# The last step of a masked-autoencoder loss: 32 sums as a row on one partition instead of a column on 32

## The chip, the cores and the metric

The kernel runs on one core of a Trainium2 chip. A core has five engines that work at the same time, each with its own queue of instructions: TensorE (PE in the profile; its weight loads are PEld), VectorE (DVE), ScalarE (ACT), GpSimd (POOL) and SyncE (SP). DMA transfers between the chip's main memory (DRAM) and the on-chip memory SBUF run on sixteen DMA engines; an instruction on SyncE or GpSimd starts them. SBUF, and PSUM, into which TensorE writes, have 128 partitions (rows). The metric is the device time of one execution in microseconds (us).

## The reference

`pred` and `target` are float32 of shape (32, 147, 768): 32 batches of 147 masked patches.

```python
mean = target.mean(axis=-1, keepdims=True)
var = target.var(axis=-1, keepdims=True)
target = (target - mean) / np.sqrt(var + 1e-6)
loss = np.mean((pred - target) ** 2, axis=-1)
return loss.mean(axis=-1).astype(np.float32)
```

The output is 32 float32 numbers, one mean for each batch, 128 bytes in all. The inputs are 28.9 MB.

## The kernel before, in words

The 147 patches of a batch are spread over four partitions, so that 32 batches fill 128 partitions. Each partition takes 37 consecutive patches, except that a batch's fourth partition takes 36. So there are 36 chunks in which all 128 partitions hold a patch (chunk c is the c-th patch of every partition), and one more, the rest, in which 96 partitions do.

Loads (line 89) bring one, two or four chunks at a time. The first two of `target` go through SyncE's queue in float32, all others through GpSimd's, which turns them into bfloat16 on the way. Then, for each chunk:

- `stats` on VectorE gives mean and variance of each patch (lines 140 and 141); ScalarE takes a square root (142), and VectorE makes the factor `r` and the offset `nmr` of it (143, 144);
- `normalise` on GpSimd writes the normalised target `s` (158);
- `subtract` on TensorE forms `p - s` in PSUM as two products with the identity and the negated identity (178). It works on units: the rest, then 17 pairs of chunks, then the last two chunks one by one. PSUM has two buffers `z` for this;
- `square` on ScalarE squares a unit in place and adds up each partition's row (184). The sum goes into one column of `rl` (128 partitions x 19 units), or into `rl_rest` for the rest.

What is left is to add, for each batch, its four partitions and its 19 columns. `mask` is 128 x 32: it holds 1/(147*768) where partition and batch belong together, and 0 elsewhere; `mask_rest` is the same for the 96 partitions of the rest. `sums` (188, 190) multiplies them on TensorE into one PSUM tile `acc`. The first fifteen columns go in one product, as soon as they are there (the early sums), then the rest, then the four last columns one by one, added to column 0 of `acc`:

```python
pin(nc.tensor.matmul(acc[:, 0:b - a], mask, rl[:, a:b], start=a == 0, stop=b == len(main_units)))
```

In `matmul(out, w, x)` the operand `w` is loaded into the array and `x` is streamed through it; the result has a partition for each column of `w` and a column for each column of `x`. So `acc` has 32 partitions and 15 columns. VectorE adds up its columns into `ob` (line 224), 32 partitions of one number, and SyncE stores them (line 225). The lines at the end of the program (256) are closing waits that the framework adds: every engine waits until all DMAs have landed.

The order in which an engine gets its instructions is set by a plan in the code: a small model of landing times and engine speeds gives each step a due time, and the steps are written out in that order and kept in it (`pin`). The plan puts the early sums and the rest's at 71.78 (three units after the square of the last of those columns), between the square of the pair (32, 33) at 70.78 and that of chunk 34 at 72.43; the last statistics stand at 63.60.

Of the kernel before, what the change touches and what calls it, by code (L numbers as in the profile page):

```python
# [7 lines left out]
F32 = mybir.dt.float32  # L8
BF16 = mybir.dt.bfloat16
ALU = mybir.AluOpType  # L10
# [4 lines left out]
def kernel(  # L15
# [7 lines left out]
    nc = tc.nc  # L23
    pin = tc.keep_in_program_order
    B, N, D = pred.shape
    eps = 1e-6
    P = 128
# [4 lines left out]
    RP = B * (J - 1)  # L32
# [17 lines left out]
    singles = ctx.enter_context(tc.tile_pool(name="singles", bufs=1))  # L50
    psum = ctx.enter_context(tc.tile_pool(name="psum", bufs=2, space=bass.MemoryType.PSUM))
    psum1 = ctx.enter_context(tc.tile_pool(name="psum1", bufs=1, space=bass.MemoryType.PSUM))
# [52 lines left out]
    mask = singles.tile([P, B], F32)  # L105
    mask_rest = singles.tile([P, B], F32)
# [55 lines left out]
    main_units = [u for u in units if u[0] != REST]  # L162
    early = len(main_units) - 4
    rl = singles.tile([P, len(main_units)], F32)
    rl_rest = singles.tile([P, 1], F32)
    acc = psum1.tile([B, early], F32)
    zs = {}

    def subtract(u):
# [14 lines left out]
        pin(nc.scalar.activation(out=z[:n, :W], in_=z[:n, :W], func=ACTF.Square, accum_out=to))  # L184

    def sums(a, b):
        if a == "rest":
            pin(nc.tensor.matmul(acc[:, 0:1], mask_rest[:RP], rl_rest[:RP], start=False, stop=False))
        else:
            pin(nc.tensor.matmul(acc[:, 0:b - a], mask, rl[:, a:b], start=a == 0, stop=b == len(main_units)))  # L190

    dve = pool = pe = act = 0.0
    ready = {}
# [11 lines left out]
    for u in units:  # L205
        pe = max([pe, free[0]] + [ready[c] for c in u] + [land["p", c] for c in u])
        at(pe, lambda u=u: subtract(u))
        pe += 0.7 * len(u)
        act = max(act, pe + 0.3)
        at(act, lambda u=u: square(u))  # L210
        act += 0.65 * len(u) + 0.35
        free = [free[1], act]
        i = main_units.index(u) if u in main_units else -1
        if i == early - 1:
            at(act + 3.0, lambda: sums(0, early))
            at(act + 3.0, lambda: sums("rest", None))
        elif i >= early:
            at(act + (3.1 if i < len(main_units) - 1 else 5.0), lambda i=i: sums(i, i + 1))
# [1 line left out]
    for when, order, fn in sorted(todo, key=lambda e: e[:2]):  # L220
        fn()

    ob = singles.tile([B, 1], F32)
    nc.vector.tensor_reduce(out=ob, in_=acc, axis=mybir.AxisListType.X, op=ALU.add)  # L224
    nc.sync.dma_start(out=out, in_=ob[:, 0])


# [33 lines left out]
```

## Time and profile before

| what | us |
|---|---|
| median of three runs (lowest to highest) | 81.42 (81.22 to 82.11) |
| profiled execution: its own time | 80.73 |
| profiled execution: span, first to last instruction | 79.0 |
| VectorE busy | 45.7 |
| ScalarE busy | 32.5 |
| GpSimd busy | 50.1 |
| TensorE busy, matmul | 38.7 |
| HBM read | 28.90 MB, 366 GB/s over the span |

The span is counted from the profiled execution's first instruction. A row of a timeline gives the start in us, the duration, the engine, the line of the code, the operation, what it writes and reads and how many instructions are merged, and in brackets how long the engine had been idle and what ended that. A row of the chain of waits gives start, duration and what the chain went through. `SPq` stands for SyncE's own instruction queue. In a row of groups stand, behind a bar, busy time, mean duration in ns, and the idle time before with what ended it. The granted clock of TensorE is 1.00 in the last stretch up to 76 us.

### The profile page before, as it was taken

To read this page: it belongs to the slowest core of one execution; us is meant where nothing else is said; L and a number is where in the kernel's file an instruction comes from. 1 tells how busy PE (TensorE), PEld (TensorE's weight loads), DVE (VectorE), ACT (ScalarE), POOL (GpSimd) and SP (SyncE) were. 2 spreads that over 40 slices of the span, in tenths; PEclk is the share of its full clock that TensorE was granted. 3 is DMA by queue.
4 is the path that set the end of the run, shared out by engine and by line. 5 is a ranking of instruction groups with operands and counts; after the bars stand their busy time and mean duration, and the time that the engine had idled before them with its cause. 6 is when DMAs were issued, how large, how long until landed. Compare 5 with 4: busy or idle time off the path is not lost.

```text
span 79.0 us, 602 instructions
## 1 busy us (share of the span) xinstructions
PE 38.7 (49%) x126; PEld 13.4 (17%) x126; DVE 45.7 (58%) x137; ACT 32.5 (41%) x53; POOL 50.1 (63%) x73
## 2 busy tenths in 40 slices
PE   0000330008990069985317980991399496496500
PEld 0000210001320023231102320320131031223300
DVE  0061039979799799797797089529779267000000
ACT  5000000050100590872931760583134873999700
POOL 4998802059789899897797795399779360800000
PEclk9999999999999655599965569759956999999996
DMA  0799999999999999999999999999999999990000
GB/s 0 182 412 317 311 218 218 211 218 218 211 215 218 211 216 218 211 211 218 218 211 215 218 215 209 221 215 211 205 227 202 210 210 220 199 165 4 0 0 0
DMA packets 3444, 15.43 MB, mean 195 GB/s; under 512 B 432, under 2 KB 784, under 8 KB 3312
## 3 DMA queue, kind: packets, MB, share of 16 engines
q0 software_dynamic: 3136, 13.52, 84.2%
q1 hardware_dynamic: 304, 1.87, 6.2%
q14 instruction: 3, 0.02, 0.1%
q8 instruction: 1, 0.02, 0.1%
HBM read 28.90 MB, written 0.00 MB: 366 GB/s over the span
## 4 chain that ended last, share of the span: by engine, by line
DMA 42%; DVE 31%; ACT 7%; POOL 5%; PE 4%; issue 4%; SPq 1%; ACTq 0%
DMA p<-in_pred_dram 30%; DVE st L140 23%; DMA t<-in_target_dram 12%; DVE mv L141 5%; ACT z L184 5%; POOL s L158 5%; PE z L178 4%; ACT r L142 2%; DVE r L143 1%; DVE nmr L144 1%; SPq L89 1%; POOL t L89 1%; PE acc L190 0%; DVE ob L224 0%; ACTq L256 0%
## 5 line engine op out<-in xcount | busy, mean ns | idle before, releaser
L140 DVE BATCH_NORM_STATS2 st<-t 128x6 f32<-128x384 bf16 (+2 forms) x74 | 36.3, 533 | 14.4 <-DMA t<-in_target_dram 14.4
L158 POOL TENSOR_SCALAR s<-t,r,nmr 128x768 bf16<-128x768 bf16 (+2 forms) x37 | 35.9, 976 | 13.3 <-DVE nmr L144 13.0
L178 PE MATMUL z<-s,nident 128*128 128x512 bf16 (+3 forms) x57 | 21.4, 492 | 26.6 <-POOL s L158 23.7
L184 ACT ACTIVATE z<-z 128x1536 f32<-128x1536 f32 (+2 forms) x20 | 26.7, 1336 | 2.0 <-PE z L178 2.0
L178 PE MATMUL z<-p,ident 128*128 128x512 bf16 (+3 forms) x57 | 20.6, 478 | 8.9 <-DMA p<-in_pred_dram 8.9
L142 ACT ACTIVATE r<-mv,eps_t 128x4 f32<-128x4 f32 (+2 forms) x12 | 3.6, 296 | 39.4 <-DVE mv L141 39.4
L178 PEld LDWEIGHTS <-nident 128*128 128x128 bf16 (+1 forms) x57 | 5.8, 117 | 39.5 <-ACT z L184 16.3
L89 POOL DMA_DIRECT2D p<-in_pred_dram x13 | 7.7, 594 | 5.2 <-DMA t<-in_target_dram 3.2
L178 PEld LDWEIGHTS <-ident 128*128 128x128 bf16 (+1 forms) x57 | 7.0, 123 | 20.5 <-issue 17.8
L141 DVE BATCH_NORM_AGGREGATE mv<-st 128x2 f32<-128x12 f32 (+1 forms) x37 | 7.7, 208 | 1.3
L89 POOL DMA_DIRECT2D t<-in_target_dram x9 | 5.3, 589 | 0.0
L143 DVE RECIPROCAL r<-r 128x4 f32<-128x4 f32 (+2 forms) x12 | 2.1, 172 | 4.6 <-ACT r L142 4.6
L224 DVE TENSOR_REDUCE ob<-acc 32x1 f32<-32x15 f32 x1 | 0.2, 161 | 7.9 <-PE acc L190 7.9
L184 ACT ACTIVATION_READ_ACCUMULATOR z<-z 128x1 f32 (+1 forms) x20 | 3.7, 186 | 0.0
L144 DVE SCALAR_TENSOR_TENSOR nmr<-mv,r 128x4 f32<-128x4 f32 (+2 forms) x12 | 1.9, 161 | 0.4
L142 ACT ACT_TABLE_LOAD x1 | 1.3, 1283 | 0.8 <-PEq L242 0.8
L190 PE MATMUL acc<-rl,mask 128*32 128x1 f32 (+1 forms) x10 | 0.8, 179 | 0.8 <-ACT z L184 0.8
L190 PEld LDWEIGHTS acc<-rl,mask 128*32 128x32 f32 x10 | 0.5, 110 | 1.5 <-ACT z L184 0.9
L110 DVE MEMSET eps_t<- 128x1 f32 x1 | 0.1, 59 | 0.9 <-PEq L242 0.9
L112 POOL MEMSET ident<- 128x128 bf16 x1 | 0.4, 362 | 0.0
L113 POOL TENSOR_SCALAR_AFFINE_SELECT ident<-ident 128x128 bf16<-128x128 bf16 x1 | 0.3, 292 | 0.1
L113 POOL TENSOR_SCALAR_AFFINE_SELECT nident<-nident 128x128 bf16<-128x128 bf16 x1 | 0.3, 292 | 0.1
(13 smaller groups left out, 2.0 us busy)
## 6 DMA issues: line engine op xcount, KB each, us to landing
t<-in_target_dram POOLq DMA_DIRECT2D x7, 768.0 KB, 26.0
p<-in_pred_dram POOLq DMA_DIRECT2D x7, 768.0 KB, 26.6
t<-in_target_dram SPq DMA_DIRECT2D x1, 1536.0 KB, 9.7
p<-in_pred_dram POOLq DMA_DIRECT2D x3, 384.0 KB, 21.8
t<-in_target_dram POOLq DMA_DIRECT2D x2, 384.0 KB, 25.9
p<-in_pred_dram POOLq DMA_DIRECT2D x2, 192.0 KB, 16.4
t<-in_target_dram SPq DMA_DIRECT2D x1, 288.0 KB, 3.7
p<-in_pred_dram POOLq DMA_DIRECT2D x1, 144.0 KB, 3.7
```

The source lines that it names most:

```text
L89: pin(eng.dma_start(out=til[:n], in_=dram(x, c0, c1)))
L112: pin(nc.gpsimd.memset(til, 0.0))
L113: pin(nc.gpsimd.affine_select(out=til, in_=til, compare_op=ALU.not_equal, fill=v, base=0, pattern=[[-1, P]], channel_multiplier=1))
L140: pin(nc.vector.bn_stats(out=st[:n, j, :], in_=til[:n, o + j * half:o + (j + 1) * half]))
L141: pin(nc.vector.bn_aggr(out=mv[:n, i], in_=st[:n]))
L142: pin(nc.scalar.activation(out=r[:n], in_=mv[:n, :, 1], func=ACTF.Sqrt, bias=eps_t[:n], scale=1.0))
L143: pin(nc.vector.reciprocal(out=r[:n], in_=r[:n]))
L144: pin(nc.vector.scalar_tensor_tensor(out=nmr[:n], in0=mv[:n, :, 0], scalar=-1.0, in1=r[:n], op0=ALU.mult, op1=ALU.mult))
L158: pin(nc.gpsimd.tensor_scalar(out=s[:n, so:so + D], in0=til[:n, o:o + D], scalar1=r, scalar2=nmr, op0=ALU.mult, op1=ALU.add))
L178: pin(nc.tensor.matmul(z[:n, a:b], w[:n, :n], src[:n, so + a:so + b], start=first, stop=not first))
L184: pin(nc.scalar.activation(out=z[:n, :W], in_=z[:n, :W], func=ACTF.Square, accum_out=to))
L190: pin(nc.tensor.matmul(acc[:, 0:b - a], mask, rl[:, a:b], start=a == 0, stop=b == len(main_units)))
```

## The change

The product with the mask is turned around: the column of sums is loaded as the weight and the mask is streamed. The result then has one partition and 32 columns. Since a weight with fifteen columns would give fifteen partitions, the fifteen early columns are first added up on VectorE into one column `rl_sum`, and the first product waits for that. The last step on VectorE becomes a plain copy of one row from PSUM to SBUF, and the store reads one partition.

```diff
-    acc = psum1.tile([B, early], F32)
+    rl_sum = singles.tile([P, 1], F32)
+    acc = psum1.tile([1, B], F32)
...
         if a == "rest":
-            pin(nc.tensor.matmul(acc[:, 0:1], mask_rest[:RP], rl_rest[:RP], start=False, stop=False))
+            pin(nc.tensor.matmul(acc, rl_rest[:RP], mask_rest[:RP], start=False, stop=False))
+        elif a == 0:
+            pin(nc.vector.tensor_reduce(out=rl_sum, in_=rl[:, 0:b], axis=mybir.AxisListType.X, op=ALU.add))
+            pin(nc.tensor.matmul(acc, rl_sum, mask, start=True, stop=False))
         else:
-            pin(nc.tensor.matmul(acc[:, 0:b - a], mask, rl[:, a:b], start=a == 0, stop=b == len(main_units)))
+            pin(nc.tensor.matmul(acc, rl[:, a:b], mask, start=False, stop=b == len(main_units)))
...
-    ob = singles.tile([B, 1], F32)
-    nc.vector.tensor_reduce(out=ob, in_=acc, axis=mybir.AxisListType.X, op=ALU.add)
-    nc.sync.dma_start(out=out, in_=ob[:, 0])
+    ob = singles.tile([1, B], F32)
+    nc.vector.tensor_copy(out=ob, in_=acc)
+    nc.sync.dma_start(out=out, in_=ob[0, :])
```

## The prediction

> **What bounds the kernel now.** I read the page's totals first, then the end of the chain of waits, then everything that touches the output.
>
> ```profile
> span 79.0 us, 602 instructions
> DMA 42%; DVE 31%; ACT 7%; POOL 5%; PE 4%; issue 4%; SPq 1%; ACTq 0%
> ```
>
> The profiled execution took 80.73 us: its span of 79.0 and 1.73 around it. It lies 0.69 below the median of 81.42, so I work out a difference on this execution and apply it to the median. The first 72 us of the chain are loads and the engines that follow them, and no edit touches them. What the change can move is the end, from the last square on:
>
> ```profile
> 73.80 0.80 ACT z L184
> 74.59 0.12 ACTq L256
> 74.71 0.04 issue
> 74.75 0.24 PE acc L190 x2
> 74.99 0.02 issue
> 75.02 0.16 DVE ob L224
> ```
>
> Nothing runs in parallel here: square, product, reduction, each waiting for the one before. The reduction ends at 75.18, and the span at 79.0, so 3.82 us (4.8% of the span) belong to storing 128 bytes and closing down. The instruction queue of SyncE, its waits and the landing of the store say how they divide, and a table by stretches shows that no engine works meanwhile (columns: stretch, its length, busy time of PE, PEld, DVE, ACT and POOL, granted clock, DMA share, GB/s):
>
> ```profile
> 75.20 0.37 SPq L225 DMA_DIRECT2D out_dram<-ob  x1
> SPq L256 <- DMA out_dram<-ob: 2.2, 1, 2.2
> DMA to landing us min/median/max: 2.9/2.9/2.9
> ...
> 75.18:76.06 0.88, 0.00 (x0) 0.00 (x0) 0.00 (x0) 0.00 (x0) 0.00 (x0) 1.00 0.00 0
> 76.06:76.24 0.18, 0.00 (x0) 0.00 (x0) 0.00 (x0) 0.00 (x0) 0.00 (x0) 1.00 0.13 1
> 76.24:78.10 1.86, 0.00 (x0) 0.00 (x0) 0.00 (x0) 0.00 (x0) 0.00 (x0) 0.87 0.00 0
> 78.10:79.00 0.90, 0.00 (x0) 0.00 (x0) 0.00 (x0) 0.00 (x0) 0.00 (x0) 0.50 0.00 0
> ```
>
> Landing is at 75.20 + 2.9 = 78.10. So 0.88 us pass from the reduction's end to the first packet (0.37 of them the issue), 0.18 with packets moving, 1.86 with no packet moving and SyncE waiting, and 0.90 of closing down. The 1.86 us is the largest piece. The DMA queues between 76.0 and 76.4 (each digit is 0.01 us) show what was sent:
>
> ```profile
> DMA  0000000232100121211011000000000000000000
> DMA packets 48, 0.00 MB, mean 0 GB/s; under 512 B 48, under 2 KB 48, under 8 KB 48
> q1 hardware_dynamic: 48, 0.00, 5.8%
> ```
>
> Forty-eight packets: 32 words and 16 more, one completion for each of 16 DMA engines. Is 1.86 us what any DMA needs from its last packet to its landing? The last load answers: its issue, its size and time to landing, and the packet counts of 71.7 to 71.8 and of 71.8 to 72.4:
>
> ```profile
> 57.23 0.58 POOL L89 DMA_DIRECT2D p<-in_pred_dram  x1
> p<-in_pred_dram POOLq DMA_DIRECT2D x1, 192.0 KB, 14.9
> DMA packets 1, 0.00 MB, mean 0 GB/s; under 512 B 1, under 2 KB 1, under 8 KB 1
> DMA packets 0, 0.00 MB, mean 0 GB/s; under 512 B 0, under 2 KB 0, under 8 KB 0
> ```
>
> It landed at 57.23 + 14.9 = 72.1, and its last packet went before 71.8: 0.3 to 0.4 us. The store takes 1.5 us more than that. The trace also records when each of the store's sixteen completions was counted; no view prints these, so I list them apart:
>
> ```
> 76.39 76.40 76.42 76.43 76.44 76.45 76.46 76.47 76.50 76.51 | 76.90 77.31 77.32 77.72 78.12 78.13
> ```
>
> Ten DMA engines were confirmed within 0.3 us of the last packet, about as fast as the load. Six came later, at a distance of 0.4 us from one step to the next. That is the look of writes that stand in line for one place, and the 32 words all go to the same 128 bytes. I take it as the cause, though the trace alone does not show what they queue for.
>
> **The store.** With the row, 32 words become one packet of 128 bytes and one completion. *Issue and start*: the 0.88 is left as it is; fewer pieces can hardly lengthen it, and no row here shows a shorter one. *Packets*: one packet in place of 0.18 us of them, so -0.15. *Confirmation*: the lower bound is the load's 0.3 in place of 1.86, a gain of 1.5; the other bound is no gain, if 1.86 belongs to writing to this memory at all. Ten engines at 0.3 speak for the first. A lone write that still pays one step of 0.4 would gain 1.1. I take 1.35, nearer to the first. SyncE reaches its wait at about 78.10 - 2.2 = 75.9, so a landing at 76.4 or later counts in full, and the closing 0.90 stays behind it. Store together: -1.5, ends -0.15 and -1.65.
>
> **The last product and its copy.** These are the rows that price them, shapes kept apart:
>
> ```profile
> L190 PE MATMUL acc<-rl,mask 128*32 128x1 f32 x8 | 0.6, 175 | 0.8 <-ACT z L184 0.8
> L190 PEld LDWEIGHTS acc<-rl,mask 128*32 128x32 f32 x10 | 0.5, 110 | 1.5 <-ACT z L184 0.9 <-issue 0.6
> L190 PE MATMUL acc<-rl,mask 128*32 128x15 f32 x2 | 0.2, 192 | 0.0
> L144 DVE SCALAR_TENSOR_TENSOR nmr<-mv,r 128x4 f32<-128x4 f32 x7 | 1.1, 162 | 0.2
> L224 DVE TENSOR_REDUCE ob<-acc 32x1 f32<-32x15 f32 x1 | 0.2, 161 | 7.9 <-PE acc L190 7.9
> ```
>
> The operands change places: 32 columns are streamed instead of 1, and 1 column is loaded instead of 32. Fourteen more columns cost 192 - 175 = 17 ns, so 31 more cost about 38; the product is two instructions, the second behind the first's stream, so twice that at most, and the shorter weight load may return something of its 110. I take +0.05, ends 0 and +0.10. On VectorE a copy of 1x32 replaces a reduction of 32x15 at 161 ns. The widths 4 and 15 both take about 161, so width counts little here: +0.01, ends -0.03 and +0.04. Both are on the path.
>
> **The early sums.** The change adds one VectorE reduction of 128x15 and makes the first product wait for it. This is the stretch, by engine:
>
> ```profile
> 66.98 0.16 DVE L144 SCALAR_TENSOR_TENSOR nmr<-mv,r 128x2 f32<-128x2 f32 x1
> 69.48 0.18 ACT L184 ACTIVATION_READ_ACCUMULATOR z<-z 128x1 f32 x1
> 72.18 0.23 PE L190 MATMUL acc<-rl,mask 128*32 128x15 f32 x2
> 72.26 0.20 PE L188 MATMUL acc<-rl_rest,mask_rest 96*32 96x1 f32 x2
> 72.64 0.19 ACT L184 ACTIVATION_READ_ACCUMULATOR z<-z 128x1 f32 x1
> 72.88 0.50 PE L178 MATMUL z<-s,nident 128*128 128x512 bf16 x2 [0.42 <-ACT z L184]
> 73.63 0.35 PE L190 MATMUL acc<-rl,mask 128*32 128x1 f32 x6
> 74.75 0.22 PE L190 MATMUL acc<-rl,mask 128*32 128x1 f32 x2 [0.77 <-ACT z L184]
> ```
>
> VectorE's last instruction before the final reduction ends at 67.14. In the code's own plan the early sums stand at 71.78 and the last statistics at 63.60, so nothing but the final copy is queued behind the new reduction on VectorE. The fifteenth pair's sum is there at 69.66; the reduction (0.16 to 0.2) is done by about 69.9, and TensorE asks for it at 72.18, so it is hidden with 2.3 us to spare. Queued behind that product on TensorE are the rest's product and the subtraction of the last chunk, which waits for a free buffer until 72.88 anyway. If the cover were gone because the reduction waited for the pair whose sum ends at 72.83, the subtraction would begin near 73.4 and all after it 0.5 later. Against that: the present product reads the same columns at 72.18, before that sum is written, so waits go by columns. The three single products at 73.63 have 1.1 us before the last one; longer streams (six times 0.04) fit. Cost of this part: 0.
>
> **Sum.** -1.5 + 0.05 + 0.01 = -1.44: the profiled execution at 79.3, the median at 81.42 - 1.44 = 80.0 us.
>
> **A rule against it.** The Trainium skill, "DMA: Bandwidth & Descriptors", section "Anatomy of one DMA — SWDGE (gpsimd) path", gives a fixed cost of about 2.0 us per DMA that scales with nothing and is mostly the write receipt of the target memory, heaviest for HBM. By that the wait would stay and the sum would be near no change, which is the first rival below; the trace agrees with it by the 1.86 us and disagrees by the ten early completions and by the load's 0.3.
>
> **The rivals.**
> *The wait is the memory's own.* Any write to the output needs 1.86 us to be confirmed by its slowest part; then only packets are saved: -0.15 + 0.06 = -0.09, or 81.3 us. For it: the trace has no other store, and the sixteenth completion is what counts. Against it: ten early ones, and the even steps. Chance 0.16.
> *It isn't one packet.* The row may be cut into 16 pieces of 8 bytes, one for each DMA engine; sixteen writes still meet in the same 128 bytes. With half of the four steps left it gains 0.8, with all of them 0; in the middle 81.42 - 0.4 = 81.0. For it: the store before uses all 16 engines. Against it: the two ends have no outer dimension left to divide. Chance 0.17. The same Trainium skill page, section "Why a DMA increments its semaphore by 16 and not by 1", says that software can split a contiguous row so that it sprays over the engines; no run here shows it.
> *Slower: one DMA engine with the whole row.* If one engine's start and confirmation is the slow thing and words were merely spread over it, the row keeps 1.86 us, and SyncE's issue grows, at most to the 0.70 of a load's issue on that queue (0.33 more):
>
> ```profile
> L89 SPq DMA_DIRECT2D t<-in_target_dram x2: 588/646/703, 0.8 to 1.6; - x2
> ```
>
> That gives 81.42 + 0.33 - 0.15 + 0.06 = 81.65. It decides as soon as the confirmation saves under 0.24. Against it: the issue lasts 0.37 with 32 pieces, so fewer should not lengthen it. Chance 0.05, the hidden reduction coming onto the path included.
>
> **How the numbers follow.** The forecast has 0.62. Its own range, from the ends of confirmation (gain 1.1 to 1.5) and product, is 79.6 to 80.4 and with the 0.2 by which the runs before lie under their median 79.5 to 80.6. To leave out no more than 2 in 10 the range must reach the first rival, so 79.5 to 81.4. One per cent, 0.81 us, is about what a measurement of this kernel tells from no change. Faster by more: 0.57 of the forecast's chance and 0.04 of the second rival's, 0.61. Within it: the rest of those, the first rival and nearly all of the third, 0.35. Slower: 0.04.
>
> **What would show it.** In the profile after: 2 packets instead of 48 at the end and a time to landing of 1.2 to 1.6 instead of 2.9 (right); 2.7 to 2.9 with 2 packets (first rival); 32 packets (second); an issue above 0.5 (third). The last product should take 0.25 to 0.32 from start to the copy, the new reduction should stand near 69.7, and the last chunk's subtraction still 0.05 us behind the end of the square before it. What would make it wrong: a lone write to this memory that is confirmed no faster than sixteen in line.

## The result, and the profile after

The changed kernel takes 78.94 us (median of four; 78.89 to 79.24) where the one before takes 81.41 (81.22 to 82.11): ratio 0.969, 95% interval 0.964 to 0.975. That is a gain of 2.47 us; 1.44 was forecast, and the time lies 0.56 below the low end of the range. The profiled execution, though, took 78.99 us with a span of 77.3, against 80.73 and 79.0: only 1.74 less. So there are two things to explain: what the 1.74 are made of, and why the medians lie further apart than the profiled executions. Of two runs further down, row_words and far_4k, the profiled execution was a slow one (82.72 and 80.63 us, the last square over 1 us later than in this one), so that of these two executions only the store is read.

The end of the chain of waits after the change:

```profile
73.92 0.80 ACT z L185
74.71 0.12 ACTq L261
74.83 0.04 issue
74.87 0.23 PE acc L195 x2
75.11 0.02 issue
75.13 0.18 DVE ob L229
```

It is the same chain: square, product, then the copy in the reduction's place, ending at 75.31 instead of 75.18. What has changed comes behind it. First SyncE's queue, its wait for the store, and the packets between 76.0 and 76.4; then the stretches from the copy's end on, with the columns as before:

```profile
75.33 0.30 SPq L230 DMA_DIRECT2D out_dram<-ob  x1
SPq L261 <- DMA out_dram<-ob: 0.4, 1, 0.4
DMA packets 2, 0.00 MB, mean 0 GB/s; under 512 B 2, under 2 KB 2, under 8 KB 2
```

```profile
75.31:76.06 0.75, 0.00 (x0) 0.00 (x0) 0.00 (x0) 0.00 (x0) 0.00 (x0) 1.00 0.00 0
76.06:76.08 0.02, 0.00 (x0) 0.00 (x0) 0.00 (x0) 0.00 (x0) 0.00 (x0) 1.00 0.03 0
76.08:76.39 0.31, 0.00 (x0) 0.00 (x0) 0.00 (x0) 0.00 (x0) 0.00 (x0) 1.00 0.00 0
76.39:77.30 0.91, 0.00 (x0) 0.00 (x0) 0.00 (x0) 0.00 (x0) 0.00 (x0) 0.65 0.00 0
```

Two packets (the row and its completion) instead of 48, and SyncE waits 0.4 us for the landing instead of 2.2. The bounds of the third stretch are the last packet and the moment at which the last completion was counted, which the trace records at 76.39. Before the change it records that moment at 78.13 (the prediction's list of completions ends there); the prediction's 1.86 counts to 78.10, with a landing of 2.9 that the view rounds to a tenth, and is 1.90 by the record. Side by side, by the trace's own times, for the two profiled executions:

| piece | before | after |
|---|---|---|
| last square ends at | 74.70 | 74.82 |
| product and reduction or copy | 0.48 | 0.49 |
| to the first packet | 0.89 | 0.75 |
| packets | 0.17 | 0.02 |
| confirmation: last packet to last completion | 1.90 | 0.31 |
| closing down | 0.90 | 0.90 |

From the last square on it is 4.33 us before and 2.46 after, 1.87 less; the work ahead ended 0.12 later this time, which leaves 1.75, the difference of the spans.

The added work, by groups (shapes apart) and by the timeline:

```profile
L195 PE MATMUL acc<-mask,rl 128*1 128x32 f32 x8 | 0.6, 192 | 0.8 <-ACT z L185 0.8
L195 PEld LDWEIGHTS acc<-mask,rl 128*1 128x1 f32 x8 | 0.3, 82 | 1.2 <-ACT z L185 0.9 <-issue 0.3
L229 DVE COPY ob<-acc 1x32 f32<-1x32 f32 x1 | 0.2, 178 | 5.3 <-PE acc L195 5.3
```

```profile
69.66 0.17 DVE L192 TENSOR_REDUCE rl_sum<-rl 128x1 f32<-128x15 f32 x1 [2.55 <-ACT z L185]
72.30 0.22 PE L193 MATMUL acc<-mask,rl_sum 128*1 128x32 f32 x2
```

A product of 32 columns takes 192 ns where one of 1 column took 175 and one of 15 columns also 192, its weight load 82 in place of 110, and the copy 178 in place of 161. The new reduction ends at 69.83, and TensorE comes for it at 72.30.

### The profile page after: what moved, and what is told of

Same layout as the page of the kernel before. It is cut to its first block, busy times and chain, and to the rows that moved or that the text cites. A ratio compares the mean times of both kernels' runs of the same rounds, so it can differ in the third digit from the quotient of the medians.

```text
span 77.3 us, 601 instructions
## 1 busy us (share of the span) xinstructions
PE 37.5 (49%) x124; PEld 13.1 (17%) x126; DVE 45.9 (59%) x138; ACT 32.6 (42%) x53; POOL 50.1 (65%) x73
## 3 DMA queue, kind: packets, MB, share of 16 engines
q1 hardware_dynamic: 258, 1.87, 6.5%
## 4 chain that ended last, share of the span: by engine, by line
DMA 43%; DVE 32%; ACT 9%; POOL 5%; issue 5%; PE 2%; SPq 1%; another core or an unknown queue 0%; ACTq 0%
DMA p<-in_pred_dram 30%; DVE st L140 24%; DMA t<-in_target_dram 13%; ACT z L185 7%; DVE mv L141 5%; POOL s L158 4%; PE z L179 2%; ACT r L142 2%; DVE r L143 1%; DVE nmr L144 1%; SPq L89 1%; POOL t L89 1%; PE acc L195 0%; DVE ob L229 0%
## 5 line engine op out<-in xcount | busy, mean ns | idle before, releaser
L179 PE MATMUL z<-s,nident 128*128 128x512 bf16 (+3 forms) x57 | 20.9, 480 | 28.7 <-POOL s L158 25.8
L179 PE MATMUL z<-p,ident 128*128 128x512 bf16 (+3 forms) x55 | 19.5, 470 | 8.1 <-DMA p<-in_pred_dram 7.9
L195 PE MATMUL acc<-mask,rl 128*1 128x32 f32 x8 | 0.6, 192 | 0.8 <-ACT z L185 0.8
```

Of the source, the lines that this page charges most:

```text
L179: pin(nc.tensor.matmul(z[:n, a:b], w[:n, :n], src[:n, so + a:so + b], start=first, stop=not first))
L195: pin(nc.tensor.matmul(acc, rl[:, a:b], mask, start=False, stop=b == len(main_units)))
```

## The experiments

What the forecast rested on is that the store of 32 words is confirmed late because words queue for one place in memory. The rivals: any store to this memory takes that long; or reading 32 partitions does; or sixteen completions do. In the runs below two numbers are read for each: the time from the last packet to the last completion, from the trace's own record (called confirmation), and the whole time where it was measured in turn with the kernel before. `far` is a scratch tensor in DRAM; runs that use it write zeros to the output early, by a store of one row on SyncE's queue.

**The row as 32 words (row_words).** Everything as after, but the 32 numbers lie apart on their partition:

```diff
-    ob = singles.tile([1, B], F32)
-    nc.vector.tensor_copy(out=ob, in_=acc)
-    nc.sync.dma_start(out=out, in_=ob[0, :])
+    ob = singles.tile([1, B, 2], F32)
+    nc.vector.tensor_copy(out=ob[:, :, 0], in_=acc)
+    nc.sync.dma_start(out=out.rearrange("(o b w) -> o b w", o=1, w=1), in_=ob[:, :, 0:1])
```

> The changed kernel, but the row's 32 numbers lie 8 bytes apart on their one partition, so that the store is again 32 words into the same 128 bytes of the output. Theory (words from several DMA engines queue up for one place in memory): time to landing 2.5 to 3.3 us as before the change, median 81.0 to 81.8. Rival (reading 32 partitions is what is slow): landing about 1.1 us, median 78.9. If the turned product itself had brought the gain, 78.9 as well, with a landing of 2.9.

Measured: 81.52 us (median of ten) beside 81.17 of the kernel before, ratio 1.0045 (1.0008 to 1.0083). The trace has 48 packets and a confirmation of 2.29 us:

```profile
76.44 0.56 SPq L230 DMA_DIRECT2D out_dram<-ob  x1
SPq L261 <- DMA out_dram<-ob: 2.8, 1, 2.8
DMA to landing us min/median/max: 3.7/3.7/3.7
```

So the turned product and the single partition bring nothing by themselves: stored as 32 words, the row loses all of the gain. The landing of 3.7 is above the 2.5 to 3.3 that I had given; 0.35 of it more than before comes ahead of the packets (the first goes 1.22 us after the issue began, and 0.86 before the change), where the issue itself now lasts 0.56 us.

**The row in 16 pieces (row_16).** The same with two numbers to a piece:

```diff
+    ob = singles.tile([1, 16, 4], F32)
+    nc.vector.tensor_copy(out=ob[:, :, 0:2], in_=acc.rearrange("p (k w) -> p k w", w=2))
+    nc.sync.dma_start(out=out.rearrange("(o k w) -> o k w", o=1, w=2), in_=ob[:, :, 0:2])
```

> The changed kernel, but the row is stored as 16 pieces of 8 bytes, one for each DMA engine, into the same 128 bytes. Theory: sixteen writes still queue, half as many as before, landing 1.7 to 2.9 us and median 79.6 to 81.0. Rival (only the number of words counts, not the engines they come from): half the excess, landing 2.0, median 80.2. Rival (many completions on one counter are what is slow): landing 2.9, median 81.4, as 32 words have as many completions.

Measured: 79.70 us beside 81.17, ratio 0.980 (0.975 to 0.985).

```profile
75.69 0.57 SPq L230 DMA_DIRECT2D out_dram<-ob  x1
SPq L261 <- DMA out_dram<-ob: 0.8, 1, 0.8
DMA to landing us min/median/max: 1.7/1.7/1.7
```

The numbers fall into the range of the theory, but not for its reason: no completion is late, and the confirmation is 0.34 us. What this run has over the row in one packet lies mostly at the start: the issue lasts 0.57 instead of 0.30, and the first packet goes at 76.91, 1.22 us after the issue began, instead of 0.73. That is 0.49 of the 0.65 us by which the stretch from the last square to the end is longer than after the change (3.12 and 2.46); another 0.14 are the packets (0.16 instead of 0.02). It also ends the rival of sixteen completions: there are sixteen here, all of them in time.

**The column to other memory (near and far_4k).** The kernel before, with its 32 words stored to `far`, side by side or 4096 bytes apart:

```diff
-    nc.sync.dma_start(out=out, in_=ob[:, 0])
+    far = nc.dram_tensor("far", (B, 1024), F32, kind="Internal").ap()   # near: (B, 1)
+    nc.sync.dma_start(out=far[:, 0], in_=ob[:, 0])
```

> The kernel before, with its column of 32 words stored to a scratch tensor of 128 bytes instead of the output; the output gets zeros early in the kernel, so the sums are left out of it. Control for the next one. Theory and both rivals: as before the change, landing 2.5 to 3.3 us, median 81.0 to 81.8. A landing of 1.1 would mean that only the output's own memory is slow.

> As the one before, with the 32 words 4096 bytes apart in the scratch tensor; the output again gets zeros early. Theory (one place): no queue, landing 1.1 to 1.4 us, median 78.9 to 79.3 (plus 0.1 for the packets). Rival (small writes are slow wherever they go): landing 2.9, median 81.4. Rival (sixteen completions are slow): landing 2.9, median 81.4.

Measured: side by side 81.14 us (80.77 to 81.36) beside 81.17, ratio 0.9986 (0.996 to 1.001); apart 79.15, ratio 0.973 (0.967 to 0.979). SyncE's wait and the landing, first side by side, then apart:

```profile
SPq L265 <- DMA far<-ob: 2.3, 1, 2.3
DMA to landing us min/median/max: 3.0/3.0/3.0
```

```profile
SPq L265 <- DMA far<-ob: 0.6, 1, 0.6
DMA to landing us min/median/max: 1.3/1.3/1.3
```

The same 32 words from the same 32 partitions through the same sixteen engines: apart they are confirmed in 0.33 us, together in 2.04. Nothing is wrong with small writes, with 32 partitions or with the memory; it is the place.

**Whose words queue (pairs_far and row_cross).** Both store the row as 32 words. In the first an engine's two words are neighbours and the pairs lie 4096 bytes apart; in the second an engine's two words lie 64 bytes apart within the output's 128:

```diff
+    far = nc.dram_tensor("far", (1, 16, 1024), F32, kind="Internal").ap()
+    nc.sync.dma_start(out=far[:, :, 0:2].rearrange("o k (h w) -> o k h w", w=1),
+                      in_=ob.rearrange("p (k h) t -> p k h t", h=2)[:, :, :, 0:1])
...
+    ob = singles.tile([1, 16, 2, 2], F32)
+    nc.vector.tensor_copy(out=ob[:, :, :, 0], in_=acc.rearrange("p (h k) -> p k h", h=2))
+    nc.sync.dma_start(out=out.rearrange("(o h k w) -> o k h w", o=1, h=2, w=1), in_=ob[:, :, :, 0:1])
```

> The changed kernel, with its row stored as 32 words to a scratch tensor: the two words that one DMA engine carries lie side by side, the pairs of the 16 engines 4096 bytes apart; the output gets zeros early, so the sums are left out of it. If what queues is one DMA engine's second word behind its own first in the same place: confirmation as before the change, 1.5 us or more from the last packet to the landing. If it is words of different engines that queue: 0.3 to 0.4 us, as with all words apart.

> The changed kernel, with its row stored as 32 words into the output's 128 bytes, in such an order that each DMA engine carries the numbers k and k + 16, 64 bytes apart; neighbouring words then come from different engines. If an engine's own pair is what queues and 64 bytes are apart enough: 0.3 to 0.4 us from the last packet to the landing. If words of different engines queue in one place: 1.5 us or more.

Measured: 0.34 us and 2.22 us (79.82 and 81.58 us for the whole, one execution each, beside one of 81.32 of the kernel before). An engine's second word does not wait for its own first. Which engine carries which word is read from the order of the pattern in the code; the trace shows 48 packets and 16 completions in both runs, but not the engine of a packet.

**One engine alone (one_engine).** If words of different engines are needed for the queue, 31 words from one engine have none:

```diff
+    far = nc.dram_tensor("far", (31, 1), F32, kind="Internal").ap()
+    nc.sync.dma_start(out=far[:, 0], in_=ob[:31, 0])
```

> The kernel before with 31 of its 32 words stored side by side to a scratch tensor; 31 has no divisor, so that one DMA engine should carry them all (32 packets instead of 48); the output gets zeros early. If words queue only behind words of other engines: 0.3 to 0.4 us from the last packet to the landing. If more than sixteen writes to one place are too many, whoever sends them: 1.5 us or more. If all of them came through one engine and each took 0.4 us: over 10 us.

Measured: 32 packets, and a confirmation of 2.16 us:

```profile
76.53 0.21 SPq L234 DMA_DIRECT2D far<-ob  x1
77.24:77.43 0.19, 0.00 (x0) 0.00 (x0) 0.00 (x0) 0.00 (x0) 0.00 (x0) 1.00 0.09 1
77.43:79.58 2.15, 0.00 (x0) 0.00 (x0) 0.00 (x0) 0.00 (x0) 0.00 (x0) 0.54 0.00 0
```

So the theory as I had it for these runs falls in one point: words of different engines are not needed for a late confirmation. What counts seems to be how many writes go to one place, whoever sends them; that also explains why sixteen pieces passed. This part is argued, not shown: 31 words from one engine far apart were not tried, so it stays possible that one engine needs this long to confirm 31 words wherever they go.

**How many, and how large a place (cross_8, far_64, words_24, words_20, apart_8).** Eight engines with two words each in 64 bytes; then the column before with its 32 words 64 bytes apart, with 24 and 20 of them side by side, and with 32 words 8 bytes apart. Each was executed once:

```diff
+    far = nc.dram_tensor("far", (1, 16), F32, kind="Internal").ap()          # cross_8, after's row
+    nc.sync.dma_start(out=far.rearrange("o (h k w) -> o k h w", h=2, w=1), in_=ob[:, :, :, 0:1])
...
+    far = nc.dram_tensor("far", (n, step), F32, kind="Internal").ap()        # the others
+    nc.sync.dma_start(out=far[:, 0], in_=ob[:n, 0])   # (32, 16), (24, 1), (20, 1), (32, 2)
```

> The changed kernel with the first 16 of its numbers stored as words to a scratch tensor of 64 bytes by 8 DMA engines, two words each that lie 32 bytes apart (24 packets); the output gets zeros early, the other 16 sums go nowhere. If a place takes sixteen writes at once and further ones queue: 0.3 to 0.4 us from the last packet to the landing. If it is an engine's second write that queues when other engines have written the place meanwhile: late steps, 0.7 us or more.

> The kernel before with its column of 32 words stored to a scratch tensor, the words 64 bytes apart (2048 bytes in all); the output gets zeros early, so the sums are left out of it. If a place for which words queue is 64 bytes or smaller: 0.3 to 0.4 us from the last packet to the landing, as at 4096 bytes. If it is larger (512 bytes, say): late steps of 0.4 us remain, 0.8 us or more.

> The kernel before with 24 of its 32 words stored side by side (96 bytes) to a scratch tensor; the output gets zeros early, so the sums are left out of it. If about sixteen writes to one place of 128 bytes pass at once and each pair beyond them takes a step of 0.42 us: 8 beyond, three to four steps fewer than with 32, 0.9 to 1.4 us from the last packet to the landing. If 32 is just over a limit that 24 keeps: 0.3 to 0.4 us.

> The kernel before with 20 of its words stored side by side (80 bytes) to a scratch tensor; the output gets zeros early. If about sixteen writes pass at once: 4 beyond, one or two steps, 0.6 to 0.9 us from the last packet to the landing. If the limit lies above 20: 0.3 to 0.4 us.

> The kernel before with its 32 words stored 8 bytes apart (256 bytes in all) to a scratch tensor; the output gets zeros early. If the place is 128 bytes or less, each takes sixteen writes and none queues: 0.3 to 0.4 us from the last packet to the landing. If it is 256 bytes or more, or the number of words in one DMA is what counts: 1.9 to 2.3 us as with words side by side.

When each completion was counted, in ns after the last packet, from the traces' record (one_engine and cross_8 have fewer engines; counts that SyncE adds at the issue are left out):

```
before      160  171  183  195  206  218  230  241  267  279 |  663 1074 1086 1486 1887 1899
before_2    166  177  189  201  212  224  236  247 |  480  920  932 1373 1816 1827 2268 2280
before_3    162  173  186  198  209  221  233  244  276 |  716  728 1165 1177 1879 2320 2332
words_24    195  217  227  237  247  257  267  277  287 |  723 1160 1170
words_20    251  261  271  281  291  301  311  321  352  362
far_64      157  170  180  190  200  210  220  230  240  250  260  270  280  290  300  323
apart_8     171  181  191  201  211  221  231  241 |  427  437 1109 1548 1558 1994 2143 2434
cross_8     267  277  287  297  307  317  327  337
one_engine 2158
```

Sixteen words in 64 bytes and twenty in 80 pass without a late step; 24 in 96 bytes have two steps of 0.44; 32 in 128 bytes have four to five, and for 31 from one engine only the end is counted, at 2.16. My figure of about sixteen for the limit was too low: words_24's 1.17 fell into the range that I had worked out from it, but words_20 has no late step where it gave one or two. By these single executions the limit lies from 20 to 23. The place is not the 128 bytes either, since 32 words over 256 bytes queue as well (2.43, above the 1.9 to 2.3 given). At 64 bytes apart they do not. A place of 256 bytes would hold 4 of those words, one of 1024 bytes 16, both within the limit, so its size stays open between them. The Trainium skill, "DMA: Bandwidth & Descriptors", section "Specifications", says that a DMA engine reads, changes and writes back where a transfer is under 512 bytes. A place of that size would fit all runs, but no run shows what the queue is made of, and the row's 128 bytes, also below 512, are confirmed in 0.31.

**Before again (before_2 and before_3).** Unchanged copies, for the gap between the profiled execution and the median:

> The kernel before once more, unchanged, for a second look at how long its store is confirmed. The timed executions of before lay 0.7 us above the profiled one of the prediction. If the number of late steps differs from execution to execution: another landing than 2.9 us, up to 3.7, and the execution's time moves with it. If the store is always the same and the loads differ: landing 2.9 again, and the last square ends elsewhere than at 74.70.

> The kernel before a third time, with the same two expectations: either the time to landing differs from 2.9 us and the execution's time moves with it, or the landing is 2.9 and the last square ends elsewhere than at 74.70.

Measured: 81.11 and 81.44 us, beside 80.73 in the execution that the prediction was made on. The last square's end and the landing, first before_2, then before_3:

```profile
74.51 0.19 ACT L184 ACTIVATION_READ_ACCUMULATOR z<-z 128x1 f32 x1
SPq L256 <- DMA out_dram<-ob: 2.6, 1, 2.6
DMA to landing us min/median/max: 3.3/3.3/3.3
```

```profile
74.80 0.19 ACT L184 ACTIVATION_READ_ACCUMULATOR z<-z 128x1 f32 x1
SPq L256 <- DMA out_dram<-ob: 2.6, 1, 2.6
DMA to landing us min/median/max: 3.4/3.4/3.4
```

The first has its square at the same 74.70 and lands 0.37 later, and that is the whole 0.38 by which it is slower. The second lands 0.42 later after the issue, and its square ends 0.29 later, together the 0.71. So both expectations hold in part: the confirmation was about 0.4 us longer in both of these executions, and the work ahead of it varies a little.

**After again, in turn with before (after_2).**

> The changed kernel once more, unchanged, timed in turn with the one before on one chip. If the store of before is confirmed in about 2.3 us in most executions, and that of the row always in 0.3: before 81.1 to 81.4, this 78.8 to 79.1, a ratio of 0.970 to 0.975, and this one's runs within 0.4 us of each other. If the profiled execution of before was typical and the 2.5 us came from a chip or an hour: before near 80.7, ratio about 0.978.

Measured: 78.93 us (six runs, 78.81 to 79.08) beside 81.08 (eleven, 80.80 to 81.52), ratio 0.973 (0.970 to 0.976); the 81.08 lies just under the 81.1 to 81.4 given. The row's confirmation was 0.32, and 0.31 the first time. The changed kernel's runs lie within 0.27 us of each other, those of before within 0.72. The varying steps may be what widens that spread, but this is not shown: row_16's four runs lie within 0.52 (79.48 to 80.00), and its profiled execution has no late completion. No version tried is faster than the changed kernel.

## Why the prediction was wrong, point by point

The sign, the place and the mechanism were right, the size was not, and the range missed. By its own steps:

- **Confirmation, forecast -1.35: mis-sized.** In the profiled pair it was -1.59 (1.90 to 0.31). I had left one late step of 0.4 as possible for a lone write, and taken a value between; the row pays none. The bound that I had from the load, 0.3, was the value.
- **From the profiled execution to the median: the step that failed most.** I took the difference of one execution and applied it to the median of 81.42, though the execution lay 0.69 below that median. The piece that the change removes is itself what varies: 1.90 us in that execution by the trace's record, 2.28 and 2.33 in the next two. With 2.3 in place of 1.90 the confirmation alone gives -2.0. The six late completions in steps of 0.4 were in the prediction, and they should have said that another execution may have more of them. The low end of the range, with at most 1.5 for the confirmation and 0.2 for the spread of the runs, left this out.
- **Issue and start, forecast 0:** -0.14 (0.89 to 0.75), of which 0.07 is the issue, 0.30 instead of 0.37.
- **Packets, forecast -0.15:** -0.15.
- **Product and copy, forecast +0.06:** +0.01. I had reckoned 38 ns for 31 more columns by extending the step from 1 to 15 columns; it was 17 ns, the same as for 15. The weight load is shorter (82 instead of 110 ns), and the chain's piece is 0.23 where it was 0.24; the copy has 17 ns more than the reduction.
- **The new reduction, forecast 0:** 0. It ends 2.47 us before TensorE comes for it, close to the 2.3 predicted.
- **Sums that do not come out.** From the ends given, the forecast's own range is 79.74 to 80.31, where the text has 79.6 to 80.4; the third rival's terms add up to 81.66, not 81.65; and the shares for "within one per cent" add up to about 0.38, not 0.35. None of them explains the miss.

Confirmation, start, packets and product give -1.59 - 0.14 - 0.15 + 0.01 = -1.87 for the end of the profiled execution. With 2.3 us for the confirmation before, it is 2.27, which lies between the 2.15 measured in turn on one chip (81.08 to 78.93) and the 2.47 of the first comparison. So of the 1.03 us between the forecast 1.44 and the measured 2.47, 0.43 were missing in the pair of executions itself, about 0.40 are the longer confirmation of the other executions (known from two of them), and 0.20 stay open. How much of the rest is the work ahead of the store was not separated.

The first rival (the memory's own wait) falls with far_4k and far_64; the second (16 pieces) did not happen, and when it was made to happen its sixteen writes did not queue (0.34): it cost 0.76 us over one packet by the medians (79.70 and 78.94), for its start and its packets and not for its confirmation; the third (one engine slower) is wrong for the row, with an issue of 0.30 and a confirmation of 0.31. The cause named in the prediction, words standing in line for one place, is shown: the same 32 words are late side by side (2.04) and not late 4096 or 64 bytes apart (0.33 and 0.32). That they had to be words of several engines was the theory of the first experiments; one_engine speaks against it. The fixed cost of about 2.0 us that the prediction set against the change is given by the Trainium skill, "DMA: Bandwidth & Descriptors", section "Anatomy of one DMA — SWDGE (gpsimd) path", for a DMA that GpSimd issues. The row's store is issued by SyncE, and this trace shows 1.06 us for it from the start of the issue to the landing (75.33 to 76.39).

## What to carry to other kernels

When a small output is stored as single words, look at the time between the last packet and the landing and compare it with that of a load; if the store's is longer, make its bytes contiguous on one partition, so that they go as one packet, or keep words bound for one small stretch of memory few (here 20 side by side passed, 24 did not). Price what such a change removes over several executions and not from one, above all where the piece consists of steps whose number may vary. And do not cut the row on purpose: 16 pieces from one partition lengthened the start of the store by 0.49 us, more than the whole confirmation of the single packet (0.31).

## What the runs showed that I had not expected

- The queue goes by the number of writes to a stretch of memory: none late at 16 and 20 words, two steps of 0.44 us at 24, four to five at 32, with the words 4 bytes apart (1.90 to 2.33 us) and no less with 8 bytes (2.43). 64 bytes apart there is none. 31 words from one DMA engine took 2.16 us, much as 32 from sixteen. Below 32 words, and at 8 and 64 bytes apart, each figure is from one execution.
- Cutting a row on one partition lengthens the issue on SyncE: 0.30 us for one packet, 0.57 for 16 pieces, 0.56 and 0.60 for 32 words, 0.75 for 16 words from 8 engines; a column of 32 partitions took 0.33 to 0.37, and 31 words by one engine only 0.21. Shape is not all, though: in the runs with `far`, the early store of zeros, 32 numbers side by side on one partition like the changed kernel's row, took 0.48 to 0.49 us to issue at 2.2 us, right behind the issues of two loads on the same queue. For the last store, the first packet goes 0.73 us after the issue's start with one packet, 1.22 with 16 pieces. Why, no run shows.
- A product in float32 with 32 columns streamed and 1 loaded costs no more than one with 1 streamed and 32 loaded (0.23 and 0.24 us for the two instructions on the chain).
